# Token sums in a lane, one rotation table, and a new order and new paces for the projection tiles of a decoder block

## The chip, the cores and the metric

The kernel runs on one core of a Trainium2 chip. The metric is device microseconds of one execution. The names of the engines in the profile are PE (TensorE, matmuls), PEld (its weight loads), DVE (VectorE), ACT (ScalarE), POOL (GpSimd) and SP (SyncE, which here only issues transfers).

## The reference

One decoder block for 1024 tokens with 16 learned meta tokens ahead of them, 1024 wide, in float32:

```
h     = LN0([meta; x])
p     = h @ w_in + b_in         columns: u_s5 | q | k | v | o | i | f | g_s5 | g_m
y_s5  = GLU(GELU(S5(u_s5)))     32 groups of a complex diagonal recurrence
y_m   = (o * HeadNorm(mLSTM(q, k, v, i, f))) @ m_w_out     4 heads, chunkwise
mix   = sigmoid(g_s5) * y_s5 + sigmoid(g_m) * y_m
h     = LN(alpha * h + mix @ w_o)
out   = LN(alpha * h + relu(h @ w_up + b_up)^2 @ w_down)
```

S5 steps a complex state by `exp(lambda dt)`. The kernel takes eight tokens as one block, so that a table of the powers of `p8 = exp(8 i Im(lambda) dt)` (the rotations, cosine and sine) serves the recurrence over the 130 blocks.

## The kernel before

Every float32 matmul is made of three terms on split operands: high × high, low × high and high × low (`mm3`, lines 226 to 228). A raw weight tile is loaded by SP (`load_w`); ACT copies it to `whi` (L212) and DVE subtracts to `wlo` (L213). PE works in order: it cannot pass a matmul whose `whi` is late.

The kernel runs in stages. First LN0, whose instructions follow an order written out by hand (`LN0_PROG`, `ln0_pipe`); it leaves the normalised tokens, transposed and split, in `hT_hi` and `hT_lo` (L1294). Then the projection tiles in the order of the string `ORDER`: `q` (a head's q and k), `v`, `u` (S5's input), `o` (output gate; `o0` and `o1` need head 0 of the mLSTM), `g` and `m` (parts of the two gates). Then the eight gated tiles z0 to z7 (`glu_job`), 48 matmuls each, which join GLU and the S5 gate in `z2s` and `sgs` (L944, L945). Then a seven-product scheme (`Seven`) for the rest of the gates and for the mLSTM's output projection; it needs sums of the four token blocks (`raw_block`, L991, `sub`, L1002) and splits its weights in L1042 and L1043. Last come w_o, LN1 and the feed-forward stage.

Work that is not a projection runs in lanes: generators that stop at each `yield n`. `pump` adds to a clock for the matmuls issued (`mm3` calls it), and a lane goes on when the clock has passed its stop by n. So the paces decide after how many matmuls the next piece of a lane stands in the program. A scheduler then orders each engine's instructions, largely by that program order. The lanes are `ml` (gates of the mLSTM, then `mlstm(h)` with `A`, `B` and the norm `N`), `cv`, `s5c` (`s5_pre`, then four `s5_consts`), `s5` (four `s5_batch`), `s5g` (gelu) and `ah`: `ah_scale` scales the residual rows `ahr` and stores them (L1386, L1388), and `up_early` behind it loads three pairs of feed-forward tiles, makes sums of them (L1394 to L1397) and splits 21 pieces (L1412 on ACT, L1413 on DVE) that SP stores (L1414) and POOL loads again much later. Before an `o` tile, `ml` is stepped until its head is ready; after z7, all lanes are drained, that is, run to their end, before `first()` splits the first product's weight.

The pool `slot` has 30 buffers of one size, shared by the weights, the lanes' tiles and the token blocks; a buffer is free when its last reader is done, a store included.

Of the kernel before, what the change touches and what calls it, by code (L numbers as in the profile page):

```python
# [9 lines left out]
F32 = mybir.dt.float32  # L10
F32R = mybir.dt.float32r
I32 = mybir.dt.int32
AF = mybir.ActivationFunctionType
# [27 lines left out]
ORDER = "q0 q1 v0 q2 v1 q3 o1 o0 v2 o2 o3 u0 u1 v3 u2 g0 u3 g1 o4 o5 o7 o6 g2 g3 g5 g6 g4 g7 m0 m1"  # L41
S5_START = "u0"
# [70 lines left out]
def decoder_block(  # L113
# [30 lines left out]
    lanes = {"ml": Lane(), "cv": Lane(), "s5": Lane(), "s5c": Lane(), "s5g": Lane(), "ah": Lane()}  # L144
# [434 lines left out]
    def s5_pre():  # L579
# [15 lines left out]
        yield 1.3  # L595
# [7 lines left out]
        yield 1.3  # L603
# [13 lines left out]
        yield 1.3  # L617
# [18 lines left out]
        yield 1.3  # L636
# [6 lines left out]
        yield 1.3  # L643
# [16 lines left out]
        yield 1.3  # L660
# [9 lines left out]
        yield 1.3  # L670
# [3 lines left out]
    def s5_consts(b):  # L674
# [311 lines left out]
    def raw_block(dr, kh, ch, off=0):  # L986
        ts = [slot("rawb"), slot("rawb")]
# [155 lines left out]
    def gates_and_output():  # L1143
# [9 lines left out]
        def first():  # L1153
            for i in range(3):
                g.load(i)
# [922 lines left out]
```

## Time and profile before

| what | value |
|---|---|
| median of 3 runs | 1549.32 us (1548.83 to 1549.41) |
| the profiled execution | 1548.64 us |
| its span, first to last instruction | 1546.8 us |
| mean granted clock of TensorE | 0.988 |

A profile's groups and waits name engine, program line and the tiles, `out<-in`. "L228 <- DVE wlo L213" is a PE instruction of line 228 that waited for line 213 on DVE. A window's row has its two ends, the length and the busy time of each engine with the number of instructions in brackets.

### The profile page before, as it was taken

How to read it: one execution, taken by the hardware profiler on the slowest of the kernel's cores; microseconds unless marked ns; L12 is line 12 of the kernel's file. 1: busy time of each engine (PE TensorE's matmuls, PEld its weight loads, DVE VectorE, ACT ScalarE, POOL GpSimd, SP SyncE). 2: the span in 40 equal slices, each digit the busy share in tenths (PEclk: the TensorE clock that was granted, in tenths of full speed). 3: DMA queues.
4: the chain of work that ended last, by engine and by line, in shares of the span. 5: the costliest groups of instructions: out<-in, count | busy, mean ns of one | idle time of the engine just before them, and what ended most of it. 6: DMA issues, size and time to landing. Idle time of an engine off the chain costs nothing.

```text
span 1546.8 us, 20543 instructions
## 1 busy us (share of the span) xinstructions
PE 1508.0 (97%) x7593; PEld 1275.0 (82%) x7593; DVE 1080.9 (70%) x2083; ACT 643.8 (42%) x982; POOL 97.7 (6%) x195
## 2 busy tenths in 40 slices
PE   8999999997999999989999999999999999999996
PEld 8999998996878888868788887888888888888886
DVE  7677555659767865659688675766666689767785
ACT  6524444334354443435543243444444534433430
POOL 0000001124021200000000001000000000000000
PEclk9999999998999999999999999999999999999998
DMA  8513224413354677756272238544443897767642
GB/s 314 166 53 95 67 73 136 117 49 91 117 118 115 172 258 232 283 192 224 82 241 72 83 110 275 176 149 148 150 147 134 275 383 283 242 223 236 201 175 96
DMA packets 122149, 261.19 MB, mean 169 GB/s; under 512 B 14568, under 2 KB 36784, under 8 KB 122048
## 3 DMA queue, kind: packets, MB, share of 16 engines
q1 hardware_dynamic: 111344, 233.00, 44.1%
q0 software_dynamic: 10704, 26.88, 7.3%
q8 instruction: 60, 0.98, 0.3%
q14 instruction: 41, 0.34, 0.1%
HBM read 188.78 MB, written 84.55 MB: 177 GB/s over the span
## 4 chain that ended last, share of the span: by engine, by line
PE 30%; issue 24%; DMA 2%; DVE 1%; SPq 0%; POOL 0%; ACT 0%; POOLq 0%; DVEq 0%
PE mm L228 7%; PE mm L227 7%; PE mm L226 7%; PE sd L227 3%; PE sd L226 3%; PE sd L228 3%; DMA wpre<-wu_dr 1%; DMA rawb<-h_dr 1%; DVE wlo L1043 0%; SPq L991 0%; DMA woraw<-in_wo_dram 0%; POOL wpre L1621 0%; DVE hT_lo L1141 0%; DVE yp L1121 0%; DVE rawb L1002 0%
## 5 line engine op out<-in xcount | busy, mean ns | idle before, releaser
L226 PE MATMUL mm<-hT_hi,whi 128*128 128x512 f32 (+3 forms) x604 | 230.2, 381 | 6.3 <-ACT whi L1042 3.8
L228 PE MATMUL mm<-hT_hi,wlo 128*128 128x512 f32 (+3 forms) x604 | 226.6, 380 | 6.3 <-DVE wlo L213 3.8
L227 PE MATMUL mm<-hT_lo,whi 128*128 128x512 f32 (+3 forms) x604 | 228.4, 378 | 0.0
L228 PEld LDWEIGHTS mm<-hT_hi,wlo 128*128 128x128 f32 x604 | 114.9, 190 | 25.8 <-DVE wlo L213 4.2
L226 PEld LDWEIGHTS mm<-hT_hi,whi 128*128 128x128 f32 x604 | 115.2, 191 | 24.6 <-ACT whi L1042 4.6
L227 PEld LDWEIGHTS mm<-hT_lo,whi 128*128 128x128 f32 x604 | 115.1, 191 | 17.6 <-issue 0.4
L1777 ACT ACTIVATE dwh<-wdr 128x1024 fp32r<-128x1024 f32 x56 | 58.9, 1054 | 86.6 <-DMA wdr<-in_wdn_dram 31.0
L227 PE MATMUL sd<-dwl,dah 128*128 128x512 f32 x240 | 94.5, 394 | 0.0
L228 PE MATMUL sd<-dwh,dal 128*128 128x512 f32 x240 | 94.4, 394 | 0.0
L226 PE MATMUL sd<-dwh,dah 128*128 128x512 f32 x240 | 94.2, 393 | 0.0
L1773 ACT ACTIVATE dah<-da 128x1024 fp32r<-128x1024 f32 x56 | 58.7, 1052 | 83.6 <-PE sd L227 37.1
L1774 DVE TENSOR_TENSOR dal<-da,dah 128x1024 fp32r<-128x1024 f32 x56 | 68.2, 1219 | 24.0 <-ACT dah L1773 23.5
L228 PE MATMUL mm<-dwh,dal 128*128 128x512 f32 (+1 forms) x224 | 84.5, 378 | 0.0
L226 PE MATMUL mm<-dwh,dah 128*128 128x512 f32 (+1 forms) x224 | 84.4, 377 | 0.0
L227 PE MATMUL mm<-dwl,dah 128*128 128x512 f32 (+1 forms) x224 | 84.3, 377 | 0.0
L1778 DVE TENSOR_TENSOR dwl<-wdr,dwh 128x1024 fp32r<-128x1024 f32 x56 | 68.2, 1219 | 12.7 <-ACT dwh L1777 11.9
L213 DVE TENSOR_TENSOR wlo<-wraw,whi 128x1024 fp32r<-128x1024 f32 (+1 forms) x46 | 56.1, 1221 | 26.7 <-ACT whi L212 20.8
L226 PE MATMUL mm<-whi,hT_hi 128*128 128x256 f32 (+1 forms) x256 | 74.3, 290 | 0.0
L228 PE MATMUL mm<-whi,hT_lo 128*128 128x256 f32 (+1 forms) x256 | 74.0, 289 | 0.0
L227 PE MATMUL mm<-wlo,hT_hi 128*128 128x256 f32 (+1 forms) x256 | 73.0, 285 | 0.0
L228 PE MATMUL mm<-th,wul 128*128 128x512 f32 x156 | 61.6, 395 | 0.0
L227 PE MATMUL mm<-tl,wuh 128*128 128x512 f32 x156 | 61.5, 394 | 0.0
(474 smaller groups left out, 3688.0 us busy)
## 6 DMA issues: line engine op xcount, KB each, us to landing
da<-act_dr SPq DMA_DIRECT2D x56, 512.0 KB, 5.5
wdr<-in_wdn_dram SPq DMA_DIRECT2D x56, 512.0 KB, 6.7
wur<-in_wup_dram SPq DMA_DIRECT2D x32, 512.0 KB, 4.4
act_dr<-upy SPq DMA_DIRECT2D x64, 256.0 KB, 2.5
wraw<-in_wf_dram SPq DMA_DIRECT2D x30, 512.0 KB, 5.3
wu_dr<-wpre SPq DMA_DIRECT2D x21, 512.0 KB, 4.9
wpre<-wu_dr POOLq DMA_DIRECT2D x21, 512.0 KB, 5.1
act_dr<-upx SPq DMA_DIRECT2D x32, 256.0 KB, 3.1
```

The source lines that it names most:

```text
L213: todo.append(lambda e=v_, r=r, hi=hi, lo=lo, n=n: e.tensor_tensor(lo[:, :n], r[:, :n], f32(hi[:, :n]), op=OP.subtract))
L226: t_.matmul(ps, ah, bh, start=(i == 0 and part[0]), stop=False, skip_group_check=skip)
L227: t_.matmul(ps, ah, bl, start=False, stop=False, skip_group_check=skip)
L228: t_.matmul(ps, al, bh, start=False, stop=(i == n - 1 and part[1]), skip_group_check=skip)
L1773: a_.activation(ah[:, :D], a[:, :D], AF.Copy)
L1774: v_.tensor_tensor(alo[:, :D], a[:, :D], f32(ah[:, :D]), op=OP.subtract)
L1777: a_.activation(wh, raw[i], AF.Copy)
L1778: v_.tensor_tensor(wl, raw[i], f32(wh), op=OP.subtract)
```

## The change

The order of the projection tiles and all paces are set anew; `s5_pre` starts at v1 instead of u0; `ah_scale` and `up_early` start at z1 instead of g4, with paces of 4 instead of 1.5 and 0.9. `s5_table` makes one rotation table of 66 columns for all 16 columns of q; a batch copies its part and adds 64 columns with one complex multiplication, instead of eight doubling steps of its own. Two of the three subtractions ahead of the first product and the move of their result to its home run in a new lane `gp` from z2, and the fourth (with block 21) stays after z7; the first product's weight tiles are loaded at z6, from a pool that now opens at z1. The software DMAs' descriptor memory is set to 4096. PE's instructions are the same in number and kind.

```diff
-ORDER = "q0 q1 v0 q2 v1 q3 o1 o0 v2 o2 o3 u0 u1 v3 u2 g0 u3 g1 o4 o5 o7 o6 g2 g3 g5 g6 g4 g7 m0 m1"
-S5_START = "u0"
+ORDER = "q0 q1 v0 v1 g0 o1 q2 v2 q3 o3 u0 u1 o0 m0 u2 g5 o2 o4 o5 u3 v3 m1 g7 g6 g2 g4 g1 g3 o6 o7"
+S5_START = "v1"
 NM = 2
 SPLIT_UP = 200
 PRE = 3
 ZD = 1
-ML = [2.4, 1.2, 1.68, 4.8]
-NL = [0.88, 1.75, 1.75, 1.75]
-C5 = [0.7, 0.98, 1.96, 0.49]
-K5 = [1.7, 3.4, 1.7, 1.7]
-Z5 = [1.0, 1.0, 1.0, 1.0]
-D5 = [2.88, 1.22, 1.44, 1.44]
-W5 = [2.21, 1.56, 2.6, 2.6]
-Y5 = [1.97, 2.82, 3.38, 2.82]
+ML = [2.87, 1.8, 1.8, 2.49]
+NL = [4, 1.69, 1.5, 2.01]
+C5 = [1.7, 2.25, 2.77, 1.57]
+K5 = [4.0, 2.0, 2.0, 4.56]
+Z5 = [2.84, 1.51, 1.42, 1.08]
+D5 = [6.15, 1.99, 3.44, 2.0]
+W5 = [2.01, 3.11, 2.33, 1.5]
+Y5 = [3.07, 2.77, 3.44, 1.8]
 AFT = 0
+AH_START = "z1"
+AHY = 4
+UPY = 4
+PRY = 1.0
+TBY = 1.69
+GY = 8.0
+GS = 4.0
...
-            r = slot("wraw") if ring[0] is None else ring[0].tile([P, 1024], F32, tag="wr", bufs=3, name="wraw")
+            r = slot("wraw")
...
+    def s5_table():
+        S5["T"] = T = mid.tile([P, 2, 16, 66], F32, name="s5_T")
+        tm, (c, s) = slot("s5tt"), (T[:, 0], T[:, 1])
+        g_.memset(c[:, :, 0], 1.0)
+        g_.memset(s[:, :, 0], 0.0)
+        g_.tensor_copy(c[:, :, 1], S5["p8"][:, 0])
+        g_.tensor_copy(s[:, :, 1], S5["p8"][:, 1])
+        yield TBY
+        n = 1
+        while n < 65:
+            m = min(n, 65 - n)
+            sh = [P, 16, m]
+            cmul(v_, c[:, :, n + 1:n + 1 + m], s[:, :, n + 1:n + 1 + m], c[:, :, 1:m + 1], s[:, :, 1:m + 1],
+                 c[:, :, n:n + 1].to_broadcast(sh), s[:, :, n:n + 1].to_broadcast(sh),
+                 *(tm[:, i * 512:i * 512 + 16 * m].rearrange("p (q c) -> p q c", q=16) for i in range(2)))
+            n *= 2
+            yield TBY
 
...
-        T = slot("s5T")
+        T, tmp = slot("s5T"), slot("s5tt")
+        t1, s1 = S5["T"][:, 0, q0:q0 + 4], S5["T"][:, 1, q0:q0 + 4]
         tc_, ts_ = (T[:, i * 520:(i + 1) * 520].rearrange("p (q c) -> p q c", q=4) for i in range(2))
-        tmp = slot("s5tt")
-        g_.memset(tc_[:, :, 0], 1.0)
-        g_.memset(ts_[:, :, 0], 0.0)
-        g_.tensor_copy(tc_[:, :, 1], S5["p8"][:, 0, q0:q0 + 4])
-        g_.tensor_copy(ts_[:, :, 1], S5["p8"][:, 1, q0:q0 + 4])
+        a_.activation(tc_[:, :, 0:66], t1, AF.Copy)
+        a_.activation(ts_[:, :, 0:66], s1, AF.Copy)
+        sh = [P, 4, 64]
+        cmul(v_, tc_[:, :, 66:130], ts_[:, :, 66:130], t1[:, :, 2:66], s1[:, :, 2:66],
+             t1[:, :, 64:65].to_broadcast(sh), s1[:, :, 64:65].to_broadcast(sh),
+             *(tmp[:, i * 512:i * 512 + 256].rearrange("p (q c) -> p q c", q=4) for i in range(2)))
         yield C5[b]
-        n = 1
-        while n < 129:
-            m = min(n, 129 - n)
-            sh = [P, 4, m]
-            w1 = tmp[:, 0:4 * m].rearrange("p (q c) -> p q c", q=4)
-            w2 = tmp[:, 512:512 + 4 * m].rearrange("p (q c) -> p q c", q=4)
-            cmul(v_, tc_[:, :, n + 1:n + 1 + m], ts_[:, :, n + 1:n + 1 + m], tc_[:, :, 1:m + 1], ts_[:, :, 1:m + 1],
-                 tc_[:, :, n:n + 1].to_broadcast(sh), ts_[:, :, n:n + 1].to_broadcast(sh), w1, w2)
-            n *= 2
-            yield C5[b]
...
-    def raw_block(dr, kh, ch, off=0):
-        ts = [slot("rawb"), slot("rawb")]
+    def raw_block(dr, kh, ch, off=0, in_ring=False):
+        ts = [ring[0].tile([P, 1024], F32, tag="rb", bufs=2, name="rawb") if in_ring else slot("rawb") for _ in range(2)]
...
         for i in range(2):
             v_.tensor_tensor(dst[i][:, :1024], a[i][:, :1024], b[i][:, :1024], op=OP.subtract)
+            yield GS
+
+    def now(steps):
+        for _ in steps:
+            pass
...
-            r = ring[0].tile([P, 1024], F32, tag="wr", bufs=3, name="wraw")
+            r = ring[0].tile([P, 1024], F32, tag="wr", bufs=4, name="wraw")
...
+        def token_sums():
+            R["12"], R["22"] = raw_block(h_dr, 0, 1, META), raw_block(h_dr, 1, 1, META)
+            R["11"] = raw_block(h_dr, 0, 0, META, True)
+            yield GY
+            yield from sub(R["22"], R["12"], R["22"])
+            yield from sub(R["12"], R["12"], R["11"])
+            yield from sub(R["11"], R["11"], R["22"])
+            to_home(R["11"], h01)
+
         def begin():
-            for nm, kh, ch in (("12", 0, 1), ("22", 1, 1), ("11", 0, 0), ("21", 1, 0)):
-                R[nm] = raw_block(h_dr, kh, ch, META)
-
-        def first():
+            lanes["gp"].drain()
+            R["21"] = raw_block(h_dr, 1, 0, META)
+
+        def early():
             for i in range(3):
                 g.load(i)
+
+        def first():
             g.split(0)
-            sub(R["22"], R["12"], R["22"])
-            sub(R["12"], R["12"], R["11"])
-            sub(R["11"], R["11"], R["22"])
-            to_home(R["11"], h01)
-            sub(R["21"], R["21"], R["11"])
+            now(sub(R["21"], R["21"], R["11"]))
             R.pop("11")
 
...
                 v_.tensor_tensor(r[:, :D], r[:, :D], gb[i][:, :D], op=op)
-                yield 1.5
+                yield AHY
...
                 nc.sync.dma_start(wu_dr[p, n - 1], f32(o[:, 0:1024]))
-                yield 0.9
+                yield UPY
...
         if j.tag == S5_START:
             lanes["s5c"].add(s5_pre())
+            lanes["s5c"].add(s5_table())
         if j.tag and j.tag[0] == "o":
             while int(j.tag[1:]) not in HMREADY:
                 lanes["cv"].drain()
                 lanes["ml"].step()
-        if j.tag == "g4":
+        if j.tag == AH_START:
             lanes["ah"].add(ah_scale())
             lanes["ah"].add(up_early())
-        if j.tag == "z7":
+        if j.tag == "z1":
             mid_ctx.close()
             ring_ctx = ExitStack()
             ring[0] = ring_ctx.enter_context(tc.tile_pool(name="ring", bufs=1, side="left"))
+        if j.tag == "z2":
+            lanes["gp"].add(token_sums())
+        if j.tag == "z6":
+            early()
+        if j.tag == "z7":
             begin()
...
+    nc = _bacc.Bacc("TRN2", target_bir_lowering=False, num_devices=1, dynamic_dma_scratch_size=4096)
```

Three places show how the instructions move (in the rows of the change the line numbers are its own).

ACT at the end of z7, before: `wpre` are the split pieces of `up_early`, `z2s` the gated tiles' evacuations, and the last row is the first product's weight copy.

```order
L1412 ACTIVATE wpre<-wur 128x512 x2
L1412 ACTIVATE wpre<-wus 128x512
L1412 ACTIVATE wpre<-wur 128x512
L1412 ACTIVATE wpre<-wus 128x512 x2
L1412 ACTIVATE wpre<-wur 128x512
L940 ACTIVATE z2s<-mm 128x512
L212 ACTIVATE whi<-wraw 128x1024
L940 ACTIVATE z2s<-mm 128x512 x3
L997 ACTIVATE hT_hi<-rawb 128x2x512
L1042 ACTIVATE whi<-wraw 128x1024
```

ACT at the same place, changed: first where the copies begin, behind z7's last `z2s`, then where they end.

```order
L957 ACTIVATE z2s<-mm 128x512
L219 ACTIVATE whi<-wraw 128x1024
L957 ACTIVATE z2s<-mm 128x512 x3
L1441 ACTIVATE wpre<-wur 128x512 x2
L1441 ACTIVATE wpre<-wus 128x512
```

```order
L1441 ACTIVATE wpre<-wur 128x512
L1441 ACTIVATE wpre<-wus 128x512 x2
L1441 ACTIVATE wpre<-wur 128x512
L1064 ACTIVATE whi<-wraw 128x1024
L1102 ACTIVATE sgm<-mm 128x512
L1064 ACTIVATE whi<-wraw 128x1024
```

The copies of `up_early` lay between the gated tiles' evacuations; now all 21 stand in one piece between z7's last evacuation and the first product's `whi` (L1064). On DVE the 12 sums and 21 subtractions stand in one piece at the same place.

PE at the first norm of head 0 of the mLSTM (`pt` are its transposes, `pn`, `pu`, `pk` and `pS` the chunks' matmuls, `mm` the projections), before.

```order
L228 MATMUL mm<-hT_hi,wlo 128x512
L226 MATMUL mm<-hT_hi,whi 128x512
L513 MATMUL pt<-ident,hraw 128x128 x4
L227 MATMUL mm<-hT_lo,whi 128x512
L228 MATMUL mm<-hT_hi,wlo 128x512
```

PE at the same norm, changed.

```order
L481 MATMUL pn<-v_883,sw 128x257
L484 MATMUL pu<-v_883,kw 128x257
L520 MATMUL pt<-ident,hraw 128x128 x2
L465 MATMUL pk<-ident,kT 128x128
L520 MATMUL pt<-ident,hraw 128x128 x4
L470 MATMUL pS<-qT,kT 128x128
L520 MATMUL pt<-ident,hraw 128x128 x2
L480 MATMUL pn<-C,qi 128x257
L481 MATMUL pn<-v_883,sw 128x257
L484 MATMUL pu<-v_883,kw 128x257
L470 MATMUL pS<-qT,kT 128x128
L233 MATMUL mm<-hT_hi,whi 128x256
```

The chunks and the norm stood between projection matmuls; now this piece and three chunks ahead of it follow one another, up to the first matmul of tile o1.

DVE in LN0 (`s_` names are S5's first step, 128x16 each; `hT_lo` is the low part of the tokens, `x_133` a group of rows), before.

```order
L1251 TENSOR_SCALAR x_120<-x_120,mv_142,y_147 128x1024
L1277 TENSOR_SCALAR hf<-ln_346,ln0t 128x256
L1241 SCALAR_TENSOR_TENSOR u_152<-mv_142,y_147 128x1
L1277 TENSOR_SCALAR hf<-ln_348,ln0t 128x256 x2
L1294 TENSOR_TENSOR hT_lo<-hf,hT_hi 128x4x256
L1215 BN_STATS st_424<-x_133 128x6
L288 MEMSET cpre 128x3
L1294 TENSOR_TENSOR hT_lo<-hf,hT_hi 128x4x256
```

DVE at the same place, changed.

```order
L565 TENSOR_SCALAR s_t_1235<-s_t_1236 128x16
L616 TENSOR_SCALAR s_kf<-s_kf 128x16
L566 TENSOR_SCALAR s_t_1235<-s_t_1235 128x16
L1323 TENSOR_TENSOR hT_lo<-hf,hT_hi 128x4x256
L1244 BN_STATS st_424<-x_133 128x6
L295 MEMSET cpre 128x3
L567 TENSOR_SCALAR s_t_1235<-s_t_1235 128x16
L618 SCALAR_TENSOR_TENSOR s_th<-s_kf,s_th 128x16
L568 SCALAR_TENSOR_TENSOR s_t_1236<-s_t_1235,s_t_1236 128x16
L1323 TENSOR_TENSOR hT_lo<-hf,hT_hi 128x4x256
```

Between the same rows of LN0 there now stand small operations of `s5_pre`; 41 of them lie in LN0's part of DVE's queue.

More of the change, by code (lines that the diff above doesn't have):

```diff
@@ L142, in row_bcast @@
         return bass.AP(tensor=src.tensor, offset=src.offset + off, ap=[[0, P], [1, n]])
-    lanes = {"ml": Lane(), "cv": Lane(), "s5": Lane(), "s5c": Lane(), "s5g": Lane(), "ah": Lane()}
+    lanes = {"ml": Lane(), "cv": Lane(), "s5": Lane(), "s5c": Lane(), "s5g": Lane(), "ah": Lane(), "gp": Lane()}
     clock = [0.0]
@@ L602, in s5_pre @@
         acc_exp(ea, a, (t1, t2))
-        yield 1.3
+        yield PRY
         r8 = t16("r8")
@@ L635, in s5_pre @@
             v_.tensor_tensor(p8[:, 0], t1, t2, op=OP.subtract)
-        yield 1.3
+        yield PRY
         for n in (1, 2, 4):
@@ L659, in s5_pre @@
         v_.tensor_tensor(wi, wi, inv, op=OP.mult)
-        yield 1.3
+        yield PRY
         sh = [P, 16, 16]
@@ L1189, in run @@
             y.run(lambda c, p: sdps() if c == "b" and p else mmps(), ym_evac, yhooks)
-        return begin, first, run
+        return token_sums, early, begin, first, run
     def ln0_load(t):
@@ L1467, in decoder_block @@
     next(ws)
-    begin, first, run7 = gates_and_output()
+    token_sums, early, begin, first, run7 = gates_and_output()
     for i, j in enumerate(jobs):
```

17 lines of the change are left out of this document (8 added, 9 removed).

## The prediction

> **What bounds the kernel now.** First the page's list of busy time: TensorE is busy 97% of the span, and the change leaves its instructions as they are, so only its waits and its slow clock can go or come. The profiled execution took 1548.64 us, 0.68 under the median of 1549.32.
>
> ```profile
> span 1546.8 us, 20543 instructions
> PE 1508.0 (97%) x7593; PEld 1275.0 (82%) x7593; DVE 1080.9 (70%) x2083; ACT 643.8 (42%) x982; POOL 97.7 (6%) x195
> ```
>
> Next, stretch by stretch, the view of windows; its second column is the length, then PE, PEld, DVE, ACT and POOL, and behind them the granted clock. I take as the loss of a stretch its length less PE's busy time, plus (1 − clock) × length.
>
> ```profile
> 300.00:350.00 50.00, 48.32 (x352) 46.46 (x351) 31.89 (x101) 14.37 (x34) 11.17 (x28) 1.00 0.19 57
> 350.00:375.00 25.00, 19.25 (x95) 14.94 (x93) 23.80 (x82) 11.55 (x19) 8.08 (x5) 0.91 0.37 107
> 375.00:400.00 25.00, 22.86 (x137) 21.82 (x138) 22.12 (x72) 10.16 (x17) 11.85 (x19) 0.88 0.50 149
> 450.00:475.00 25.00, 22.68 (x99) 18.02 (x98) 14.81 (x46) 16.05 (x20) 1.48 (x2) 0.93 0.33 67
> 500.00:525.00 25.00, 23.83 (x132) 20.00 (x131) 21.03 (x72) 10.73 (x20) 9.06 (x18) 1.00 0.52 157
> 600.00:650.00 50.00, 50.00 (x218) 40.58 (x217) 34.87 (x53) 19.39 (x31) 0.00 (x0) 1.00 0.73 253
> 650.00:700.00 50.00, 43.86 (x180) 34.59 (x179) 32.05 (x34) 19.84 (x25) 0.00 (x0) 0.93 0.62 220
> ```
>
> The losses are 1.7, 8.0, 5.1, 4.1, 1.2, 0 and 9.6 us: 20.1 between 300 and 525, and 9.6 at the end of the gated tiles. PE's own waits name what is late there:
>
> ```profile
> PE mm L228 <- DVE wlo L213: 3.8, 1, 3.8
> PE mm L226 <- ACT whi L1042: 3.8, 1, 3.8
> PE s5k L741 <- DVE s5Ri L719: 2.9, 1, 2.9
> PE mm L228 <- DVE wlo L1043: 2.4, 1, 2.4
> PE pt L513 <- DVE hraw L506: 1.7, 1, 1.7
> PE mm L226 <- ACT whi L212: 1.2, 1, 1.2
> PE s5y L858 <- DVE s5w L846: 1.2, 1, 1.2
> ```
>
> Between 350 and 375 VectorE is busy 23.80 of 25.00 us: S5's constants and rotation tables stand in its queue ahead of a weight split (L213). At the end of the gated tiles the chain of waits shows the token sums:
>
> ```profile
> 653.09 1.12 SPq L1414
> 658.19 8.94 DMA rawb<-h_dr
> 676.52 1.15 DVE wlo L1043
> ```
>
> The loads of the four blocks are issued late behind SP's stores of `up_early` (L1414), land after 9 us, and eight subtractions (L1002) then stand ahead of the first product's split (L1043).
>
> **The change part by part.** *Removed.* One shared table takes about 126 VectorE instructions out, the S5 lanes are spread out, and two of three token sums now run beside the gated tiles. I credit the whole 20.1 + 9.6 = 29.7 us, which is generous: nothing else in those stretches is dear.
>
> *`up_early` is left over after z7.* This is the term that decides. Before, its 21 pieces lay between the gated tiles' evacuations, where PE lost nothing (600 to 650: 50.00 busy). Now its lane starts at z1, and each of the 16 steps of `ah_scale` ahead of it waits 4 us on the lanes' clock: 16 × 4 + 6 = 70 us, about what the seven gated tiles z1 to z7 give (48 matmuls of 512 columns each, hence some 10 us). The order shows the consequence: all 21 copies on ACT, and all 12 sums and 21 subtractions on VectorE, stand behind z7's last operation and ahead of the first product's `whi` and `wlo`, and PE's next matmul needs that `whi`. PE waits for the whole of it. The prices, from the tiles' views and the DMA list:
>
> ```profile
> L1394 DVE TENSOR_TENSOR wus<-wur x16: 682/692/694, 602.4 to 1189.0; 128x512 f32<-128x512 f32 x16
> L1412 ACT ACTIVATE wpre<-wur x12: 616/632/634, 599.3 to 650.4; 128x512 fp32r<-128x512 f32 x12
> 642.51 0.69 DVE L1394 TENSOR_TENSOR wus<-wur 128x512 f32<-128x512 f32 x1 [4.23 <-DMA wur<-in_wup_dram]
> 643.24 0.69 DVE L1395 TENSOR_TENSOR wus<-wus,wur 128x512 f32<-128x512 f32 x1
> 643.85 0.69 DVE L1396 TENSOR_TENSOR wur<-wur 128x512 f32<-128x512 f32 x1
> 644.45 0.68 DVE L1397 TENSOR_TENSOR wus<-wur,wus 128x512 f32<-128x512 f32 x1
> wur<-in_wup_dram SPq DMA_DIRECT2D x32, 512.0 KB, 4.4
> ah_dr<-ahr SPq DMA_DIRECT2D x8, 512.0 KB, 3.0
> ```
>
> Such VectorE operations follow each other every 0.60 us (643.85 to 644.45). Floor, if every load were in time: 33 × 0.60 = 19.8, plus the 1.05 of `whi`: 21 us. But the loads are not in time. The first pair's buffers come free when an `ah_dr` store issued in z7 has landed (3.0), then take 4.4 to load: its sums can start about 5 us after z7's end. A pair is 4 sums and 7 subtractions, 11 × 0.60 = 6.6: done at 12. On SP the second tile of the next pair stands behind the first pair's first store (about 8.5): it lands at 13, and the pair is done at 20. The third pair's second tile stands behind the second pair's fifth store (about 19): it lands at 24; its last copy on ACT is done at 29, and `whi` at 30. I take 30 us (21 to 33), nearest to the serial reading, since SP's order is fixed. After a pause PE runs at half clock: the 3.5 us of the clock's share in 650 to 700 (0.07 × 50). So 33 with it.
>
> The Trainium skill ("TensorE: Matmul & The Clock Gate", Part 1: The HAM clock gate) says that an idle PE falls to half clock and gets the full clock back after about 3.4 us of work; by that rule alone the after-effect would be 1.7 us where the trace's stretch shows 3.5, and the sum 1.8 lower.
>
> The Trainium skill ("DMA: Bandwidth & Descriptors", Anatomy of one DMA) gives for a software-issued transfer 2.0 us plus the bytes at 436 GB/s, an estimate of 3.2 us for 512 KB; SP's loads here land in 4.4, and with 3.2 the three loads in series would shorten the wait by some 3.6 us.
>
> *The mLSTM ahead of o1.* The first output-gate tile is now the sixth job, and head 0 must be finished by then; so five chunks and the first norm of that head stand on PE in one run with no projection matmuls between them. Before has a shorter run of the kind at 451 to 462, from the timeline:
>
> ```profile
> 453.13 0.48 DVE L482 SCALAR_TENSOR_TENSOR C<-C,dec,pu 128x257 f32<-128x257 f32 x1
> 453.67 0.49 PE L463 MATMUL pS<-qT,kT 128*128 128x128 f32 x2 [0.47 <-DVE C L482]
> 453.92 1.28 ACT L172 ACT_TABLE_LOAD   x1
> 456.68 1.38 DVE L506 TENSOR_SCALAR hraw<-hraw,hmv,hny 128x256 f32<-128x256 f32 x4
> 457.15 0.44 PE L513 MATMUL pt<-ident,hraw 128*128 128x128 f32 x2 [1.68 <-DVE hraw L506]
> ```
>
> Each chunk waits about 0.5 us for its state, the norm 1.7, and half clock follows: 4.1 us in that stretch, for about two thirds of the work that now stands together. I take 4.1 × 1.5 = 6. Below, 2, if PE arrives late enough that lanes have run ahead; above, 12, with two spells of half clock and the first `whi` of o1 behind the copies of `hmF` on ACT.
>
> *S5's first step inside the first LayerNorm.* `s5_pre` is now due at v1, and the order places 41 of its 16-column operations between VectorE's rows of the first LayerNorm.
>
> ```profile
> L565 DVE SCALAR_TENSOR_TENSOR s_dt<-s_dt,s_t x6: 174/175/177, 117.3 to 118.3; 128x16 f32<-128x16 f32 x6
> 34.10 1.23 DVE L1294 TENSOR_TENSOR hT_lo<-hf,hT_hi 128x1024 fp32r<-128x1024 f32 x1 [0.24 <-ACT hT_hi L1296]
> 35.44 1.10 PE L1305 MATMUL mm<-hT_lo,whi 128*128 128x256 f32 x8
> 30.00:40.00 10.00, 10.00 (x89) 10.00 (x89) 9.55 (x17) 7.87 (x12) 0.00 (x0) 1.00 0.83 290
> ```
>
> VectorE is busy 9.55 of 10 us there, and `hT_lo` is ready at 35.33, 0.11 before PE uses it. Twelve of the small operations at 0.17 come between VectorE's idle spell before 28.3 and that row: 2.0 us late. The others follow ahead of the last group's statistics. I take 3 (0 if ACT's own waits hide them, 6 if all 29 later ones, 29 × 0.17 = 4.9, reach PE).
>
> *Buffers at the gated tiles.* The token-sum tiles, the rows of `ahr` and the gated weights now share the 30 buffers. The splits `whi` of z3 and z4 wait for PE's last use of the tile before (two matmuls ahead of the next tile, 0.5 us by the 218 matmuls in 50 us above, against 1.05 for the copy), those of z5 and z6 for an `ah_dr` store, 3.0 us by the row above. Before, PE waited for nothing there. I take 3 in all: 2 × 0.5 + 2 × 1.0 (0 if the stores land early; 8 if both wait a whole landing and z3 and z4 wait 1 each).
>
> *Edges.* The gelu ahead of z0 now waits for the last S5 batch through DRAM, and z0 for head 3's norm, where the waits of before were about 1 us each (L212, L846): I take 2 (0 to 5). The smaller descriptor memory of software DMAs I cost at nothing: POOL is busy 6%, and its transfers are issued far ahead of their use; if POOL's queue stalled, the first waits would appear at the table's small copies.
>
> Sum: 1548.64 − 29.7 + 33 + 6 + 3 + 3 + 2 = 1565.9, so **1566 us**. Against the median of before that is 17 slower.
>
> **The rivals.** *Faster: the drain finds its loads ready.* If the second and third pairs' loads land before the pair ahead is done, VectorE alone sets the drain: 21 and a half-clock spell of 1.7, and if the lanes also run ahead of PE at o1 (2) and the other new waits stay hidden, the time is 1548.64 − 29.7 + 22.7 + 2 = 1543.5. The point from which it decides: all new waits together under 29.7 us. For it speaks that DMA queues are otherwise quiet after z7; against it that SP issues in order, and that its loads stand behind stores of results not yet made.
>
> *Slower still: the new waits at their upper bounds.* VectorE nearly continuous in the first LayerNorm and both stores awaited in full: 36 + 12 + 6 + 8 + 5 − 29.7 = +37, 1586; with about half of that excess, 1578. For it speaks VectorE's 9.55 of 10 us; against it that PE's own delay gives the other engines time.
>
> *The change does not do what it says in the S5 stretch.* If the four blocks of S5 constants, which it leaves in place, and not the tables, overfill VectorE at 350 to 400, some 13 of the 20 us stay: 1566 + 13 = 1579. Against it: their order is now spread over more tiles.
>
> **How the numbers follow.** Forecast 0.56 (own range 1556 to 1575), faster rival 0.17, waits at the upper bounds 0.15, S5 stretch not relieved 0.12. What can be told from no change is 0.2%, 3 us. Of the faster rival's 0.17, 0.04 lies within 3 us; of the forecast's lower tail another 0.02. So faster 0.13, same 0.06, slower 0.81. The range goes from the faster rival to above the two slower ones: 1544 to 1582.
>
> **What would show it.** Right: a single PE wait of about 30 us on the first product's `whi` after z7, with 21 `wpre` copies on ACT and SP's waiting loads inside it; PE idle without names of DMAs between the first head's chunks before o1; no wait on `s5Ri` or on the split in the S5 stretch. Wrong: a wait after z7 under 22 us, a first LayerNorm no longer than before, or PE busy under 48 of 50 us in the S5 stretch after all. The forecast fails by its sign if the removed waits exceed the drain; it fails by size alone if the drain is right and o1, LayerNorm or buffers are off.

## The result, and the profile after

The changed kernel takes 1567.47 us (median of 4 runs, 1566.52 to 1568.07) against 1549.37 us (1548.83 to 1550.04) for the kernel before on the same chip. The ratio is 1.0116, 95% interval 1.0099 to 1.0134: it is slower by 18 us. The profiled execution took 1566.52 us, 17.9 more than that of before. Lines below are those of the changed kernel: the three matmuls are L233 to L235, the splits of a projection weight L219 and L220, those of the seven products L1064 and L1065, the pieces of `up_early` L1423 to L1443.

The head of the page, then PE's own waits (total, times, longest, in us):

```profile
span 1564.6 us, 20453 instructions
PE 1504.2 (96%) x7593; PEld 1272.5 (81%) x7593; DVE 1065.1 (68%) x1957; ACT 648.8 (41%) x991; POOL 82.0 (5%) x183
...
PE mm L233 <- ACT whi L1064: 36.0, 1, 36.0
PE ln L1290 <- ACT x L1278: 4.1, 2, 3.0
PE pS L470 <- ACT kw L467: 2.5, 4, 1.0
PE pt L520 <- DVE hraw L513: 2.3, 1, 2.3
PE mm L233 <- ACT whi L219: 1.9, 2, 1.0
```

One wait of 36.0 us, for the first weight split behind z7, is twice the whole difference. The three waits of the S5 stretch in the list of before (on `wlo`, `s5Ri` and `s5w`, 7.9 us together) are gone. The view of windows says the same by stretches; columns as in the prediction:

```profile
150.00:175.00 25.00, 21.11 (x112) 17.72 (x111) 17.02 (x63) 15.93 (x25) 1.61 (x2) 0.93 0.07 22
350.00:375.00 25.00, 25.00 (x127) 20.54 (x126) 16.79 (x40) 8.00 (x14) 1.88 (x3) 1.00 0.24 74
...
550.00:600.00 50.00, 48.98 (x217) 39.74 (x216) 25.54 (x45) 18.57 (x22) 1.45 (x2) 1.00 0.64 201
600.00:650.00 50.00, 47.94 (x205) 37.81 (x204) 32.95 (x36) 12.84 (x17) 0.00 (x0) 1.00 0.53 187
650.00:700.00 50.00, 14.01 (x60) 11.14 (x59) 34.07 (x49) 13.71 (x24) 0.00 (x0) 0.65 0.79 299
700.00:750.00 50.00, 50.00 (x212) 40.21 (x212) 36.00 (x37) 26.48 (x31) 0.00 (x0) 0.97 0.68 243
```

Between 350 and 375 VectorE falls from 23.80 to 16.79 us and PE is busy throughout, as it is from 300 to 350 and from 500 to 525. Between 650 and 700 PE works 14.01 of 50 us, while VectorE is busy for 34.07: no compute engine is near its limit. (The granted clock of 0.65 is that of a stretch in which PE mostly stands; it costs time only where PE works.) The two last columns, the share of the DMA engines and the GB/s that they move, say that these are another matter: 0.79 on average, and for the 16 us from 677 on they are full, while before, where the same pieces ran beside the gated tiles, had 0.73 from 600 to 650 with PE busy throughout.

```profile
677.00:693.00 16.00, 0.00 (x0) 0.00 (x0) 6.44 (x12) 3.86 (x7) 0.00 (x0) 0.50 1.02 413
```

The chain of waits (start, length, what):

```profile
662.93 4.69 DMA wur<-in_wup_dram
...
671.27 5.04 DMA wur<-in_wup_dram
...
684.38 0.77 SPq L1443
685.20 7.48 DMA wur<-in_wup_dram
...
698.13 0.96 ACT whi L1064
699.13 0.79 PE mm L233
...
702.48 0.41 PE mm L235
702.89 0.23 PE mm L233
```

Three times a load of `up_early` is on the chain, each followed by its pair's sums and pieces, the third time with several of SP's stores of pieces ahead of it. The wait is thus a serial chain, and its last and longest load (7.48 us) runs while the DMA engines are full. The matmuls after the pause take 0.4 us and from 702.89 on 0.23.

### The profile page after: what moved, and what is told of

Its sections match the earlier page's. It is cut to its first block, busy times and chain, and to the rows that moved or that the text cites. A ratio compares the mean times of both kernels' runs of the same rounds, so it can differ in the third digit from the quotient of the medians.

```text
span 1564.6 us, 20453 instructions
## 1 busy us (share of the span) xinstructions
PE 1504.2 (96%) x7593; PEld 1272.5 (81%) x7593; DVE 1065.1 (68%) x1957; ACT 648.8 (41%) x991; POOL 82.0 (5%) x183
## 4 chain that ended last, share of the span: by engine, by line
PE 67%; issue 16%; DMA 2%; ACT 2%; DVE 2%; SPq 0%; POOLq 0%; ACTq 0%; DVEq 0%
PE mm L233 17%; PE mm L235 17%; PE mm L234 17%; PE sd L234 3%; PE sd L235 3%; PE sd L233 3%; DMA wur<-in_wup_dram 1%; PE pn L480 1%; PE pn L481 1%; PE pu L484 1%; DMA wiB<-wrow_dr 1%; PE ln L1600 0%; PE pt L520 0%; ACT gelf L891 0%; PE s5y L874 0%
## 5 line engine op out<-in xcount | busy, mean ns | idle before, releaser
L233 PE MATMUL mm<-hT_hi,whi 128*128 128x512 f32 (+3 forms) x604 | 230.7, 382 | 36.0 <-ACT whi L1064 36.0
L235 PE MATMUL mm<-hT_hi,wlo 128*128 128x512 f32 (+3 forms) x604 | 225.3, 376 | 0.1
L233 PEld LDWEIGHTS mm<-hT_hi,whi 128*128 128x128 f32 x604 | 114.2, 189 | 55.2 <-ACT whi L1064 36.8
L235 PEld LDWEIGHTS mm<-hT_hi,wlo 128*128 128x128 f32 x604 | 114.0, 189 | 18.5 <-DVE wlo L1065 0.8
L233 PE MATMUL sd<-dwh,dah 128*128 128x512 f32 x240 | 94.1, 393 | 0.0
L235 PE MATMUL sd<-dwh,dal 128*128 128x512 f32 x240 | 94.1, 393 | 0.0
L235 PE MATMUL mm<-dwh,dal 128*128 128x512 f32 (+1 forms) x224 | 84.4, 377 | 0.0
L233 PE MATMUL mm<-dwh,dah 128*128 128x512 f32 (+1 forms) x224 | 84.4, 377 | 0.0
L233 PE MATMUL mm<-whi,hT_hi 128*128 128x256 f32 (+1 forms) x256 | 73.5, 287 | 0.0
L235 PE MATMUL mm<-whi,hT_lo 128*128 128x256 f32 (+1 forms) x256 | 73.0, 285 | 0.0
L220 DVE TENSOR_TENSOR wlo<-wraw,whi 128x1024 fp32r<-128x1024 f32 (+1 forms) x46 | 55.9, 1220 | 18.4 <-ACT whi L219 15.6
L219 ACT ACTIVATE whi<-wraw 128x1024 fp32r<-128x1024 f32 (+1 forms) x46 | 48.4, 1057 | 31.6 <-issue 7.1
L235 PE MATMUL mm<-th,wul 128*128 128x512 f32 x156 | 61.4, 394 | 0.0
```

The costliest lines, as they stand in the source:

```text
L219: a_.activation(hi[:, :n], r[:, :n], AF.Copy)
L220: todo.append(lambda e=v_, r=r, hi=hi, lo=lo, n=n: e.tensor_tensor(lo[:, :n], r[:, :n], f32(hi[:, :n]), op=OP.subtract))
L233: t_.matmul(ps, ah, bh, start=(i == 0 and part[0]), stop=False, skip_group_check=skip)
L235: t_.matmul(ps, al, bh, start=False, stop=(i == n - 1 and part[1]), skip_group_check=skip)
```

## The experiments

Each comparison is with the kernel before in the same group of runs, and ratios carry 95% intervals.

### The early pieces sooner

```diff
-AH_START = "z1"
-AHY = 4
-UPY = 4
+AH_START = "g7"
+AHY = 1.5
+UPY = 0.9
```

> The changed kernel with the residual rows and the early feed-forward pieces started at g7 instead of z1, at the paces of before (1.5 and 0.9). Theory (the leftover pieces after z7 make the loss): PE's single wait of 36.0 us for the first product's weight falls under 3 us, the half clock behind it goes too, so 1567.5 - 36 - 1.5 + about 1 = 1531 us. Rival (buffers are short, and whoever gets them early takes them from S5 and the gated tiles): new waits of 10 us or more between g7 and z7, and 1545 us or more.

1565.19 us, 1.011 (1.0095 to 1.0126): no better. The wait after z7 is gone (650 to 700: 50.00 busy), and others stand in its place, by PE's waits, the windows and a row of VectorE's timeline:

```profile
PE mm L233 <- DVE z2s L961: 8.0, 1, 8.0
...
PE mm L233 <- ACT whi L219: 5.0, 4, 4.2
...
525.00:550.00 25.00, 15.21 (x79) 12.90 (x77) 21.04 (x47) 8.40 (x12) 2.03 (x2) 0.80 0.29 87
...
600.00:620.00 20.00, 11.85 (x45) 8.93 (x45) 7.65 (x13) 5.01 (x9) 1.45 (x2) 0.84 1.03 351
...
616.35 0.69 DVE L1423 TENSOR_TENSOR wus<-wur 128x512 f32<-128x512 f32 x1 [12.32 <-DMA wur<-in_wup_dram]
```

At 600 to 620 neither VectorE nor ACT is busy for more than 8 of 20 us. The last row names the longest wait: VectorE stands 12.32 us for a load of `up_early`, with a gated tile's `z2s` queued behind it, and PE waits 8.0 us for that `z2s`. By the chain 6.80 of them are the load itself, among full DMA engines (1.03). Elsewhere the chain has a weight's split behind a store of residual rows that takes 8.43 us (from 549.50): a buffer that comes free late, and a slow transfer. The late start of the lane is thus only one way to lose those microseconds. By its numbers the rival holds (new waits, a time above 1545 us); its reason, short buffers, is not the only one at work.

### The loads by another queue

```diff
-                nc.sync.dma_start(r[j][:, :D], wup[2 * p + j].rearrange("p k f -> p (k f)"))
+                g_.dma_start(r[j][:, :D], wup[2 * p + j].rearrange("p k f -> p (k f)"))
```

> The changed kernel, with the six loads of the early pieces issued by POOL's queue instead of SP's; everything still runs after z7. Theory (the pairs run in series because their loads stand on SP behind stores of the pair ahead): the waits for the second and third pair's tiles shrink, PE's wait falls from 36.0 to 23 to 27 us, and the time to about 1557 us. Rival (the loads wait for buffers, which only the stores of the pair ahead set free, or ACT and VectorE set the pace themselves): PE's wait stays at 33 to 37 us and the time within 3 us of 1567.

1568.56 us, 1.0129 (1.0115 to 1.0143), with a wait of 35.2 us after z7. POOL's timeline has the six loads with what it stood idle for:

```profile
664.26 1.67 POOL L1433 DMA_DIRECT2D wur<-in_wup_dram  x3 [79.45 <-PE mm L235]
...
682.63 1.05 POOL L1433 DMA_DIRECT2D wur<-in_wup_dram  x2 [14.54 <-DVE wpre L1442]
```

On a queue with nothing of their own ahead of them, the last two still wait 14.54 us, by this view for a VectorE split, by the chain for the landing of a store of pieces. Both are last readers of a buffer. So they wait for a buffer to come free, and the turn behind SP's stores is not the only reason. Once issued, they meet the full DMA engines; the chain and the window:

```profile
677.19 4.90 DMA wu_dr<-wpre
...
683.16 9.79 DMA wur<-in_wup_dram
...
677.00:693.00 16.00, 0.00 (x0) 0.00 (x0) 7.56 (x14) 4.38 (x8) 1.05 (x2) 0.50 1.02 384
```

Issued 2 us earlier than in the changed kernel, the last load takes 9.79 us instead of 7.48 and lands no earlier. My reason for the chain's shape falls as the only one; the chain stays.

### The descriptor memory alone

The kernel before with one edit:

```diff
-    nc = _bacc.Bacc("TRN2", target_bir_lowering=False, num_devices=1)
+    nc = _bacc.Bacc("TRN2", target_bir_lowering=False, num_devices=1, dynamic_dma_scratch_size=4096)
```

> The kernel before with nothing changed but the descriptor memory of software DMAs, set to 4096. The closing drain of POOL took 6.50 us in the profile of before and 2.99 us in that of the change. Theory A (the smaller memory is quicker to close): the drain takes about 3.0 us, the time falls by 3.5 to 1546 us. Theory B (the drain's length comes from what ran last, not from that memory): it stays near 6.5 us, and the time at 1549.4.

1545.88 us (11 runs) against 1548.84 (15 runs), ratio 0.998 (0.9971 to 0.9988). The closing instruction of POOL, of before and then of this run (min/median/max in ns):

```profile
L2074 POOLq DRAIN  x3: 46/97/6502, 1539.5 to 1546.5; - x3
```

```profile
L2074 POOLq DRAIN  x3: 46/97/2905, 1540.5 to 1544.2; - x3
```

The gain is at the end of the program: 3.6 us of drain. In the changed kernel the same instruction takes 2990 ns. So 3.5 us of the changed kernel's time are a gain that my sum did not have.

### The sums lane alone

The kernel before, its old order, paces and tables, with the lane `gp`, the weights loaded at z6 from a pool that opens at z1, and the small descriptor memory:

```diff
+        def token_sums():
+            R["12"], R["22"] = raw_block(h_dr, 0, 1, META), raw_block(h_dr, 1, 1, META)
+            R["11"] = raw_block(h_dr, 0, 0, META, True)
+            yield GY
+            yield from sub(R["22"], R["12"], R["22"])
...
```

> The kernel before with the token sums in a lane and the first products' weights loaded at z6, as in the change, and with the small descriptor memory; order, paces and rotation tables as before. Theory (the late token sums alone made the 9.6 us at the end of the gated tiles): the waits of 3.8 and 2.4 us for the first product and the half clock behind them go, new waits for buffers at the gated tiles cost 0 to 2 us; about 9 us faster than the kernel with the small memory alone. Rival (the loads of the blocks or their sums hold PE elsewhere instead): less than 4 us faster than that kernel.

1564.0 us, 1.0103 (1.0089 to 1.0117): 18 us slower than the run above, worse than either expectation. Its PE waits and windows, from the slowest of its four executions (1567.81 us), and a row of ACT's timeline:

```profile
PE mm L233 <- ACT whi L219: 17.3, 6, 7.7
...
600.00:650.00 50.00, 42.83 (x167) 32.86 (x165) 32.19 (x43) 14.30 (x22) 0.00 (x0) 0.90 0.61 212
650.00:700.00 50.00, 38.82 (x147) 30.60 (x148) 22.75 (x32) 13.60 (x21) 0.00 (x0) 0.86 0.63 229
...
655.27 1.06 ACT L219 ACTIVATE whi<-wraw 128x1024 fp32r<-128x1024 f32 x1 [4.38 <-DMA wu_dr<-wpre]
```

The losses of the two windows are 12.2 and 18.2 us, where before lost 0 and 9.6. The last row shows a short pool at work: the split of a gated weight stands 4.38 us until a store of pieces has landed and left its buffer. That it is the token blocks that took the buffers is argued, since the run also moves the loads of the first product's weights. The lane and these loads together cost more than the stall that they take away.

### The sums after z7 again

The changed kernel with the token sums as before and the pieces from g4 on:

```diff
-AH_START = "z1"
-AHY = 4
-UPY = 4
+AH_START = "g4"
+AHY = 1.5
+UPY = 0.9
...
-            lanes["gp"].drain()
-            R["21"] = raw_block(h_dr, 1, 0, META)
+            for nm, kh, ch in (("12", 0, 1), ("22", 1, 1), ("11", 0, 0), ("21", 1, 0)):
+                R[nm] = raw_block(h_dr, kh, ch, META)
```

> The changed kernel with the token sums loaded at z7 and made after it, as before, and the residual rows and early pieces started at g4 at the paces of before (1.5 and 0.9); new order, paces, shared table, early first weights and small descriptor memory stay. Theory (the lane of sums takes the buffers that the early pieces need, and only the two together make the loss): no long wait after z7 beyond the 6 to 9 us of before, no waits for buffers at the gated tiles; 1567.5 - 37.5 - 3 + 6 to 9 = 1533 to 1536 us. Rival (the early pieces collide with S5 in the new order whatever the sums do, as the 25 us of waits between 450 and 560 in the run of early_up suggest): those waits stay, 1548 us or more.

1556.58 us, 1.0044 (1.0029 to 1.0059). The S5 stretch keeps its gain (300 to 400: 100 of 100 us busy), but the last S5 batch is late:

```profile
500.00:550.00 50.00, 40.24 (x193) 33.27 (x192) 29.22 (x73) 13.92 (x24) 1.54 (x2) 0.90 0.40 117
...
523.37 0.70 DVE L834 TENSOR_TENSOR s5w<-s5Z,s5T 128x520 f32<-128x520 f32 x1 [2.52 <-DMA ah_dr<-ahr]
```

The last row, from VectorE's timeline, shows one way in which a short pool reaches PE: VectorE stands 2.52 us for a store of `ahr` to land, with S5's and the mLSTM's operations queued behind. The DMA engines are not full in this window (0.40). The rival, that the pieces collide elsewhere, holds.

### The same with the old tables

```diff
-        T, tmp = slot("s5T"), slot("s5tt")
...
+        while n < 129:
...
+            yield C5[b]
-            lanes["s5c"].add(s5_table())
```

> As sums_after_z7, but each S5 batch makes its own rotation table with the eight doubling steps and the paces C5 of before; there is no shared table. Theory A (the new order and paces took away the 20 us of waits between 300 and 525): within 3 us of sums_after_z7, and PE busy over 48.5 of 50 us from 350 to 400. Theory B (the table took them away): 10 to 15 us slower than sums_after_z7, with a wait on the S5 constants or on a weight's low part behind them.

1548.23 us, 0.9991 (0.9982 to 1.0001), 10 runs. The paces `C5` are those of before as well.

```profile
350.00:400.00 50.00, 50.00 (x268) 41.92 (x267) 38.90 (x112) 23.16 (x37) 14.95 (x27) 1.00 0.50 138
450.00:475.00 25.00, 21.13 (x93) 16.89 (x91) 17.40 (x47) 18.80 (x25) 13.76 (x22) 0.89 0.46 106
500.00:550.00 50.00, 47.24 (x232) 38.61 (x231) 31.05 (x74) 18.77 (x29) 1.55 (x2) 1.00 0.45 128
```

With the eight doubling steps of each batch back, PE still does not wait between 300 and 400, where before lost 14.8 of the stretch's 20.1 us: there the new order and paces suffice without the shared table. Between 450 and 475 they do not: 6.6 us are lost, against 0.1 in the run above, with a wait of 3.9 us for a weight's `wlo` that stands behind an S5 batch in VectorE's queue. What the shared table does in the old order was not run. That this kernel is also 8 us faster than with the shared table no theory expected; the difference shows at 500 to 550 (47.24 against 40.24 busy). Why is open: a batch now stops eight times on the lanes' clock instead of once and so comes at another time, and a buffer is held elsewhere; the two were not separated.

### o1 behind q2

The kernel with the sums after z7, and:

```diff
-ORDER = "q0 q1 v0 v1 g0 o1 q2 v2 q3 o3 u0 u1 o0 m0 u2 g5 o2 o4 o5 u3 v3 m1 g7 g6 g2 g4 g1 g3 o6 o7"
+ORDER = "q0 q1 v0 v1 g0 q2 o1 v2 q3 o3 u0 u1 o0 m0 u2 g5 o2 o4 o5 u3 v3 m1 g7 g6 g2 g4 g1 g3 o6 o7"
-ML = [2.87, 1.8, 1.8, 2.49]
-NL = [4, 1.69, 1.5, 2.01]
+ML = [2.0, 1.8, 1.8, 2.49]
+NL = [0.88, 1.69, 1.5, 2.01]
```

> As sums_after_z7, with o1 placed behind q2 and the first head's paces 2.0 and 0.88 instead of 2.87 and 4, so that the run of mLSTM matmuls without projections ahead of o1 falls from 28 rows to 19. Theory (each chunk in the run waits about 0.5 us, the norm 2.3, and half clock follows): the loss between 150 and 200, about 6 us, falls to 2 to 3; 3 to 4 us faster than sums_after_z7. Rival (the wait only moves to the next run of head 1): within 1.5 us of it.

1555.64 us, 1.0031 (1.0017 to 1.0046), where the run without it had 1.0044. Between 150 and 200 PE is busy 47.76 instead of 46.11 us at the same clock of 0.97. One and a half microseconds of the place come back, about one of the time, which is not clear of the noise (the two intervals overlap): the wait for head 0 is mostly still there.

### Everything moved, one buffer more

The changed kernel with o1 behind q2, 31 buffers, the pieces from g4 and the sums lane from z4:

```diff
-    big = ctx.enter_context(tc.tile_pool(name="big", bufs=30, side="left"))
+    big = ctx.enter_context(tc.tile_pool(name="big", bufs=31, side="left"))
...
-        if j.tag == "z2":
+        if j.tag == "z4":
```

> The changed kernel with 31 buffers instead of 30, the early pieces from g4 at the paces of before, the lane of token sums from z4 instead of z2, and o1 as in sums_after_z7_o1_later. Theory (buffers): the early pieces are nearly done when the sums load, so that neither waits long; no wait over 3 us at the gated tiles or after z7, 1525 to 1530 us. Rival (the blocks of the sums still push the gated tiles' splits behind stores): waits of 10 us or more from z4 on, 1538 us or more, no better than sums_after_z7.

1546.09 us, 0.9978 (0.9969 to 0.9988), 10 runs: faster than before by about the 3 us of the descriptor memory. What is left of the waits: 7.4 us on `whi` L219 in four places, and 6.4 us on ACT's operations for the mLSTM and S5 between 520 and 550; with the clock, 500 to 550 loses 14.2 us and 600 to 700 another 8.5. The time lies in the rival's range (1538 us or more), but the rival also said no better than the run with the sums after z7, and this one is 10 us faster. Neither expectation fits whole.

### The pieces between the products

The changed kernel, but the lane `ah` is run to its end behind the seven products instead of ahead of them:

```diff
-    for l in lanes.values():
-        l.drain()
+    for nm, l in lanes.items():
+        if nm != "ah":
+            l.drain()
     first()
     run7()
+    lanes["ah"].drain()
```

> The changed kernel with one edit: the lane of the residual rows and the early pieces is not run to its end after z7 but goes on at its paces through the seven products, and is run to its end behind them. Theory (the piece of work after z7 costs what it does because it stands at once ahead of the first product, in buffers that are not free; spread over the products, where buffers come free and VectorE has room, it costs nothing): PE's wait of 36 us goes, 1567.5 - 37.5 = 1530 us with at most 3 us of new waits in the products, so 1529 to 1534. Rival (it collides wherever it stands, as the starts at g7 and g4 did): waits of 10 us or more between 660 and 860, 1540 us or more.

1566.96 us, 1.0114 (1.0097 to 1.013). The wait of 36.0 us is gone (650 to 700: 46.67 busy), and the time is what it was:

```profile
700.00:750.00 50.00, 38.98 (x145) 29.59 (x146) 33.60 (x38) 22.42 (x31) 0.00 (x0) 0.86 0.39 134
750.00:800.00 50.00, 44.90 (x188) 36.07 (x187) 37.68 (x47) 22.17 (x26) 0.00 (x0) 0.97 0.60 201
800.00:850.00 50.00, 42.48 (x172) 33.06 (x171) 46.84 (x92) 28.07 (x81) 2.21 (x4) 0.93 0.73 262
...
PE mm L235 <- DVE wlo L1065: 6.5, 3, 5.1
PE sd L235 <- DVE wlo L1065: 6.4, 1, 6.4
...
703.00 3.49 DVE L1019 TENSOR_TENSOR rawb<-rawb 128x1024 f32<-128x1024 f32 x3
...
834.19 1.06 ACT L1162 ACTIVATE hT_hi<-woraw 128x1024 fp32r<-128x1024 f32 x1 [5.51 <-DMA woraw<-in_wo_dram]
```

The three windows lose 18.0, 6.6 and 11.0 us, 35.6 in all (the changed kernel: 1.5, 0.1 and 0). The cost has moved behind z7 and kept its size, as the rival had it. The waits no longer have one cause, as the last two rows, from the timelines of VectorE and ACT, show. The wait of 6.4 us is one for VectorE's order: `wlo` stands behind block subtractions (L1019), and VectorE is busy for 7.6 of the 8 us from 700. A third wait, 6.3 us for ACT's `hT_hi` of w_o's rows, comes from a load that is late while the last stores of pieces run and the DMA engines are full (1.03 from 828 to 836).

### The same with one buffer more and o1 behind q2

> As pieces_in_products, with o1 behind q2, the first head's paces 2.0 and 0.88, and 31 buffers. Theory (what is left in pieces_in_products are the 6 us ahead of o1 and 2 to 3 us of buffers at z3 and z4): 3 to 5 us faster than pieces_in_products, about 1526 us. Rival (one buffer more does not free the splits of z3 and z4, and the wait ahead of o1 only moves, as it did in sums_after_z7_o1_later): within 1.5 us of it.

1543.99 us, 0.9962 (0.9947 to 0.9977): 23 us faster than the run above, where 3 to 5, or at most 1.5, were expected. The first of the three windows:

```profile
700.00:750.00 50.00, 44.91 (x179) 35.07 (x177) 40.72 (x47) 28.27 (x36) 0.00 (x0) 0.93 0.48 163
```

The three lose 8.6, 2.0 and 1.6 us: 23 us less than above, some 550 us behind o1. The edit differs in two things. Moving o1 (with the first head's paces) was worth about 1 us in the other kernel, which makes the 31st buffer the likely cause of most of it. This is argued: the two were not run apart in this kernel, and VectorE's order at 700 to 708 is not the same in the two runs either.

### One buffer more, nothing else

> The changed kernel with 31 buffers in the shared pool instead of 30 and nothing else. Theory (the loads after z7 and the splits of z3 and z4 wait for buffers): the two waits of 0.96 us at the gated tiles go or shrink, and PE's wait after z7 falls from 36 to 26 to 32 us, since one load of the pairs in series starts earlier; 1556 to 1563 us. Rival (the order of the queues after z7 sets it, and a buffer more changes nothing there): PE's wait 34 to 38 us, 1565 to 1569 us.

1561.92 us, 1.0083 (1.0067 to 1.0099): 5.5 us faster than the changed kernel. By its profile (span 1560.7 us, 3.9 shorter) the wait after z7 is 34.7 us; its chain of waits and a window:

```profile
666.20 5.20 DMA wur<-in_wup_dram
...
680.34 7.89 DMA wur<-in_wup_dram
...
672.00:688.00 16.00, 0.00 (x0) 0.00 (x0) 6.23 (x11) 3.86 (x7) 0.00 (x0) 0.50 1.02 412
```

The first pair's load is no longer waited for, since it found a buffer before z7's end; the second and the third are, and the third again takes nearly 8 us in a stretch in which the DMA engines are full (1.02). In the drain one buffer is worth 1.3 us. The rest of the 3.9 lies ahead of it: 450 to 500 and 550 to 600 are busy throughout, where the changed kernel lost 1.0 in each, and 0 to 75 loses 11.7 instead of 12.6. The time came out as my theory had it, the wait as the rival had it.

### The old tables and 32 buffers

The run with the pieces between the products, 31 buffers and o1 behind q2, and in addition the per-batch tables of before, with their paces `C5`, and

```diff
-    big = ctx.enter_context(tc.tile_pool(name="big", bufs=31, side="left"))
+    big = ctx.enter_context(tc.tile_pool(name="big", bufs=32, side="left"))
...
-            r = ring[0].tile([P, 1024], F32, tag="wr", bufs=4, name="wraw")
+            r = ring[0].tile([P, 1024], F32, tag="wr", bufs=3, name="wraw")
```

> As pieces_in_products_o1_later, but each S5 batch makes its own rotation table as before; the room of the shared table goes to a 32nd buffer (with three instead of four tiles for the products' weights). Theory (buffers are dearer than VectorE's time): the waits between 600 and 850 fall below the 12 us that they have there, and the time to 1535 to 1540 us. Rival (the 126 VectorE instructions that come back hold S5 up between 300 and 560, or the fourth weight tile was needed): 1544 us or more, no better than pieces_in_products_o1_later.

1539.26 us (1537.65 to 1540.55, 5 runs), ratio 0.9938 (0.9925 to 0.9951). This version is faster than both kernels: by 10 us than before, by 28 than the changed one. The theory's range (1535 to 1540 us) came.

```profile
300.00:450.00 150.00, 148.79 (x904) 131.79 (x903) 114.00 (x350) 66.65 (x117) 39.49 (x85) 1.00 0.45 118
```

The old tables take 114.00 us of VectorE between 300 and 450 (98.60 with the shared one) and cost PE 1.2 us there. The whole is 4.7 us faster than the run with 31 buffers all the same. Its reason, that buffers are dearer than VectorE's time, is not shown by that: the old tables came back without any further buffer in the run with the sums after z7, and that was 8 us faster too.

## Why the prediction was right, point by point

**The forecast and its sum.** 1566 us was forecast; 1567.47 was measured, the profiled execution at 1566.52. The likeliest case came, with its signs and nearly its size.

**The removed 29.7 us.** The five windows of the S5 stretch lost 20.1 us before and lose 0.97 now: 19.1 gained. The 9.6 at z7's end went too, replaced by the drain. (Of the four sums ahead of the first product three, not two, run in the lane: `token_sums` calls `sub` three times.) The prediction put the S5 gain down to the table, the spread lanes and the sums together; the run with the old tables shows that order and paces suffice between 300 and 400, and that 6.6 us come back at 450 to 475 without the shared table.

**The drain, 33 us.** The wait was 36.0, not 30. The chain of the prediction, in us after z7's last matmul (662.5): first sums at 5, measured 5.1; second sums at 13, measured 13.9; third pair's load landed at 24, measured 30.2 (692.77). So the mis-sized step is the third pair: its load was issued at 685.20, 22.7 after z7 instead of 19, and took 7.48 us instead of the median 4.4. The reason given for it, SP's order, was wrong as a sole cause, since on POOL's queue the last loads waited too and landed no earlier. SP's stores of pieces were slow to issue themselves (a median of 1.05 us for 21 stores). Behind both stands what the prediction left out. It called the DMA queues quiet after z7, but the six loads and 21 stores of the drain are 27 transfers of 512 KB, 14 MB: at the 413 GB/s of the full stretch some 34 us, an estimate, with the last stores running on behind the wait. How the 36 us divide between the chain, the buffers and the DMA engines is open: no run changed the bytes.

The Trainium skill ("DMA: Bandwidth & Descriptors", Anatomy of one DMA) has 3.2 us for a software-issued transfer of this size, an estimate from its formula. The three loads on the chain, issued by SP, took 4.69, 5.04 and 7.48, and the six that POOL issued in the run with another queue 4.4 to 9.8 us, so with other transfers under way the traces do not agree.

**The half clock behind it, 3.5 us.** From 699.13 to 702.89 the matmuls take 0.4 instead of 0.23 us, so about half of 3.8 us, 1.9, is lost. My share of 0.07 came from a stretch of before with two waits. The Trainium skill ("TensorE: Matmul & The Clock Gate", Part 1: The HAM clock gate) has full clock back after about 3.4 us of work; with 3.8 here the trace agrees about, and its 1.7 us was nearer than my 3.5. Wait and clock together are 37.9 us, against 33.

**The mLSTM ahead of o1, 6 us.** 150 to 175 loses 25 − 21.11 + 0.07 × 25 = 5.6, where before lost nothing. Right: three waits of 0.5 for a chunk's `kw`, 2.3 on the norm, and the clock.

**The first LayerNorm, 3 us.** The windows from 0 to 75 of before and after:

```profile
0.00:75.00 75.00, 68.50 (x538) 66.95 (x539) 51.88 (x113) 45.84 (x74) 5.48 (x17) 0.95 0.70 244
```

```profile
0.00:75.00 75.00, 67.64 (x519) 66.06 (x520) 55.14 (x174) 47.56 (x76) 3.17 (x19) 0.93 0.71 251
```

10.3 us lost before, 12.6 after: 2.4 more. The size was right, the place was not: no wait for `hT_lo` shows. PE waited for `x` of the last group (4.1 us, 3.2 before), and the granted clock fell from 0.95 to 0.93, 1.5 us over the stretch.

**Buffers at the gated tiles, 3, and edges, 2.** 600 to 650 loses 2.1: two waits of about 1 on `whi` L219, as argued for z3 and z4; the store waits of z5 and z6 did not show. 550 to 600 loses 1.0, and another 0.5 lies on an S5 matmul. That is about the 2 of the edges, but the 1.0 is a wait for the mLSTM's state (L480), not one of the two waits that were named.

**Descriptor memory, nothing.** Wrong: POOL's closing drain fell from 6.50 to 2.99 us. The sum now reads −19.1 − 9.6 + 37.9 + 5.6 + 2.4 + 2.1 + 1.5 − 3.5 = 17.3, and 17.9 was measured. A drain that was 5 us too small and a tail that was 3.5 too large nearly cancelled; that the total came out so close owes something to that.

**The rivals.** The faster one, loads that are ready, did not come: VectorE waited for a load three times (1.42, 1.93 and 9.52 us). The upper bounds did not all come together, only the drain reached its own. (Half of the excess of 1586 over 1566 would be 1576, not 1578.) That the S5 stretch would not be relieved was excluded by 350 to 400, busy throughout.

**What the prediction missed.** It took the drain after z7 as the cost of a late lane. The runs show a cost that the placing alone does not remove: pieces at g7 1565.19, after z7 1567.47, between the products 1566.96; and the sums lane with its early loads, in the kernel before, costs 18. In all of them 30 buffers are shared by one stretch's weights, residual rows, pieces and token blocks, the engines take their work in order, and the pieces' 14 MB of transfers have to fit in. The traces show each of the three as the end of some wait: a buffer that a store still held (2.52 and 4.38 us), VectorE's order (6.4 us), a load among full DMA engines (7.48 and 9.79 us). With 31 or 32 buffers and the pieces between the products the same work costs 23 to 28 us less. The buffer's share in that is argued from the runs around it, since no run changed it alone in that kernel.

## What to carry to other kernels

Where side work shares buffers, queues and DMA engines with the main work, moving it can move the wait: look in the profile first for a wait in which no compute engine is full, then at the DMA share in a window as narrow as the wait (0.79 over 50 us hid 1.02 over 16), and ask which transfer or last reader holds the buffer. A table that spares VectorE time need not pay: both runs that brought the old tables back were faster, for reasons that stay open. And a sum that comes out right should be gone through term by term, since here two errors of 5 and 3.5 us cancelled.

## What the runs showed of the hardware that I had not expected

The software DMAs' descriptor memory has a price at the end of a program: POOL's closing drain took 6.50 us with the memory as it was and 2.91 with it set to 4096, and the whole kernel 3.0 us less (ratio 0.998, 0.9971 to 0.9988). The issue of a store is not of fixed length either: SP's 21 stores of pieces took from 0.32 to 1.24 us each to issue while the transfers of one stretch ran together, with a median of 1.05 against 0.33 for the same stores in the kernel before, and the load behind them took 7.48 instead of 4.69. At the 413 GB/s of the full stretch 512 KB take 1.27 us, an estimate close to the longest issue; that the queue issues no faster than the DMA engines take is a reading of these two numbers, not tested. The rows of before and of the change:

```profile
L1414 SPq DMA_DIRECT2D wu_dr<-wpre x21: 319/327/1117, 606.2 to 653.1; - x21
```

```profile
L1443 SPq DMA_DIRECT2D wu_dr<-wpre x21: 319/1052/1239, 670.9 to 701.5; - x21
```
